# Hybrid encoder on one core: squares of the first norm on VectorE, two more banks for the third FFN tile, later constants, decays and masked scores on ScalarE

## The chip, the cores and the metric

One Trainium2 chip, one core. The metric is the device time of one execution in microseconds; three executions of the kernel before gave a median of 2577.45 us (2576.88 to 2578.72).

## What is computed

A two-layer encoder on 512 tokens of width 1024 in f32. Each layer is half an FFN, a mixer of three branches (SSD, S5, retention) with sigmoid gates, and half an FFN; every part starts with an RMS norm. From the reference, cut to what the change touches:

```
def rmsnorm(x, g):
    return x * lax.rsqrt(jnp.mean(x * x, axis=-1, keepdims=True) + EPS) * g
def swiglu(x, w_gate, w_up, w_down):
    return (jax.nn.silu(x @ w_gate) * (x @ w_up)) @ w_down
# per layer: x = x + 1/2 * swiglu(rmsnorm(x)); mixer; x = x + 1/2 * swiglu(rmsnorm(x))
# SSD, per chunk of 128 tokens and per head, each direction:
    scores = jnp.einsum('bclhn,bcshn->bhcls', cm, bm) * segsum_exp(da)
    y_diag = jnp.einsum('bhcls,bcshp->bclhp', scores, xd)
```

## The kernel before

x is kept transposed as eight tiles `x[k]` of 128 features by 512 tokens. Weights come in chunks: `wload` (L138 to L152) starts the DMA on SyncE into `wst`, ScalarE rounds it to fp32r (`whi`, L149), VectorE subtracts (`wlo`, L150); the pool has three buffers of each. `mm3` (L156 to L158) makes each product of three matmuls, high by high, high by low, low by high. The order in which each engine gets its instructions is set by the framework's scheduler from the program's text and its priorities; each engine runs its own list in order.

**The start.** `load_first` (L255) issues x and the first weights. `norm_k` (L164) scales x by the gain and splits it into `hh` (ScalarE, L170) and `hl` (VectorE, L171). `norm_sq` (L175) squares `x[k]`: k=0 on GpSimd (L180), the others on ScalarE into `sqk` (L183; tag `t_a`, three buffers), and GpSimd adds them to `sqsum` (L184). `norm_fin` (L186) splits the sum (L161, L162), sums over features by matmuls with ones (L194), takes the power on GpSimd (`rtd`, L199), scales the identity by it (`dg`, L202) and spreads it over the partitions by a matmul of ones by `dg` (L204), copied to `rbc` (L206). The `ffn` (L208) applies `rbc` only after a product: per tile m, gate and up product (24 matmuls each) go into two PSUM banks of tag "mm", which has four; then `gt` = gate product times `rbc` (L224, VectorE), Silu (L225, ScalarE), times `rbc` (L227, GpSimd), times the up product (L229, VectorE). So TensorE can do two tiles before `rbc` exists, and the third waits for a bank. `load_consts` (L124) loads `con` (identity, masks) and `tri`, casts two triangles of `tri` to fp32r (`ls_r` L131, `us_r` L133); `load_vecs2` (L277) loads small vectors and makes `hbg` (L281). The generator `side` (`s5_prep`, with the loads L712, L717, L866 on ScalarE's queue) is advanced by one step after each FFN tile, at a low priority.

**The SSD stage.** In `ssd` (L516), `stage_a(t)` makes the masked scores `gm` of a chunk t (L622, L626) and `stage_b(t)` (L640) does, per group g of four heads: `bm` = forward scores by step size (L644, GpSimd), plus the backward ones (four instructions, L647, VectorE); twice (forward, backward) `rb`, a triangle mask times the decay of each head, in a high part `dah` (L653, VectorE) and a low part `dal` (L653, GpSimd); four matmuls with `ls_r`, `us_r` (L657); Exp (`e`, L660, ScalarE); `e` by `bm` (L661, VectorE); four matmuls with `xs` (L664). There are eight such rounds a layer (four chunks, two groups). Between chunks `hook()` runs an S5 block (L997 to L1045: `za`, `zb`, scan and `h` on VectorE, `z`, `ia`, `ib` on GpSimd, products into `ps_pa`, `ps_pb`), and the gate projections (24 matmuls a tile, L1056, L1058) fill TensorE in between.

Of the kernel before, what the change touches and what calls it, by code (L numbers as in the profile page):

```python
# [101 lines left out]
class Core:  # L102
    def __init__(self, ctx, tc, consts):
# [17 lines left out]
        nc.vector.memset(self.nmh, -0.5)  # L121

    def load_consts(self):
        nc = self.nc  # L124
        nc.sync.dma_start(self.con, self.consts[:, :C_N])
        self.ones_r = self.c0.tile([P, 2], F32R, name="ones_r")
        nc.vector.tensor_copy(self.ones_r, self.ones[:, :2])
        tri = self.tp.tile([P, 2 * P], F32, tag="t_a", name="tri", bufs=3)
        nc.sync.dma_start(tri, self.consts[:, C_LS:C_LS + 2 * P])
        self.ls_r = self.c0.tile([P, P], F32R, name="ls_r")  # L130
        nc.vector.tensor_copy(self.ls_r, tri[:, :P])  # L131
        self.us_r = self.c0.tile([P, P], F32R, name="us_r")
        nc.vector.tensor_copy(self.us_r, tri[:, P:])  # L133
# [4 lines left out]
    def wload(self, src, nk, n, eng=None):  # L138
# [5 lines left out]
        for j, s_ in enumerate(srcs):  # L144
            (eng or nc.sync).dma_start(sv.rearrange("p (k n) -> p k n", k=nk)[:, :, j * wd:(j + 1) * wd],
                                       s_.rearrange("(k p) n -> p k n", p=P))
# [17 lines left out]
    def norm_k(self, k, gcol, sq=True):  # L164
# [5 lines left out]
        nc.scalar.activation(self.hh[k], x, AF.Copy, scale=g)  # L170
# [4 lines left out]
    def norm_sq(self, k):  # L175
        nc = self.nc
        x = self.x[k]
        if k == 0:
            self.sq = self.c1.tile([P, S], F32, tag="sqsum", name="sqsum")
            nc.gpsimd.tensor_tensor(self.sq, x, x, ALU.mult)  # L180
        else:
            t = self.tp.tile([P, S], F32, tag="t_a", name="sqk", bufs=3)
            nc.scalar.activation(t, x, AF.Square)  # L183
            nc.gpsimd.tensor_tensor(self.sq, self.sq, t, ALU.add)  # L184
# [23 lines left out]
    def ffn(self, ap, wg, wu, wd, after, side=iter(()), pre=None):  # L208
        nc = self.nc
        blocks = ((0, 10), (10, 22))  # L210
        for bi, (m0, m1) in enumerate(blocks):
            ah, al = [], []
            for m in range(m0, m1):
# [3 lines left out]
                pg = self.bank()  # L217
                for k in range(KD):
                    self.mm3(pg, gh[:, k], gl[:, k], self.hh[k], self.hl[k], k == 0, k == KD - 1)
                pu = self.bank()  # L220
# [33 lines left out]
    def load_first(self, i):  # L254
# [16 lines left out]
        nc.scalar.activation(warm, self.ones[:, :2], AF.Silu)  # L271
        for k in range(KD):
# [3 lines left out]
    def load_vecs2(self, i):  # L276
        nc = self.nc  # L277
        nc.sync.dma_start(self.vec2, i["vecs"][:, 108:])
        nc.sync.dma_start(self.s5d, i["s5ds"])
        self.hbg = self.c0.tile([P, 48], F32, name="hbg")  # L280
        nc.vector.tensor_scalar(self.hbg, self.vec[:, V_BG:V_BG + 48], 0.5, None, ALU.mult)  # L281
# [225 lines left out]
    def ssd(self, i, L, xs, hook=lambda: None):  # L507
# [4 lines left out]
        with self.tc.tile_pool(name="ssd", bufs=1) as sp:  # L512
# [126 lines left out]
            def stage_b(t, w_, gm):  # L639
                py = self.bank("sm")  # L640
                for g in range(2):
                    hs = slice(4 * g, 4 * g + 4)
                    bm = sp.tile([P, 4, P], F32, tag="bm", name="bm", bufs=2)
                    nc.gpsimd.tensor_tensor(bm, self.bc(gm[:, 0, g].unsqueeze(1), [P, 4, P]),  # L644
                                            self.bc(dt4[:, t, 0, hs].unsqueeze(2), [P, 4, P]), ALU.mult)
                    for h in range(4):
                        nc.vector.scalar_tensor_tensor(bm[:, h], gm[:, 1, g], dt4[:, t, 1, 4 * g + h:4 * g + h + 1],  # L647
                                                       bm[:, h], ALU.mult, ALU.add)
                    seg = self.bank("sm")
                    for d, m, lm in ((0, ui, self.ls_r), (1, li, self.us_r)):  # L650
                        rb = sp.tile([P, 2, 4, P], F32R, tag="rb", name="rb", bufs=2)
                        for j, s_ in enumerate((dah.bitcast(F32), dal)):
                            (nc.vector if j == 0 else nc.gpsimd).tensor_tensor(  # L653
                                rb[:, j], self.bc(m.unsqueeze(1), [P, 4, P]),
                                self.bc(s_[:, t, 8 * d + 4 * g:8 * d + 4 * g + 4].unsqueeze(2), [P, 4, P]), ALU.mult)
# [44 lines left out]
    def s5_params(self, i, L, keep, sp, sd):  # L700
# [9 lines left out]
        for nm in ("s5_lam_re", "s5_lam_im"):  # L710
            o = new(nm)
            nc.scalar.dma_start(o, i[nm][L])  # L712
# [3 lines left out]
        for d in range(2):  # L716
            nc.scalar.dma_start(ls[64 * d:64 * d + 64, :], i["s5_log_step"][L, d].partition_broadcast(64))  # L717
# [122 lines left out]
        with self.tc.tile_pool(name="s5c", bufs=1) as qp:  # L840
# [23 lines left out]
            for ri, nm in enumerate(("s5_c_re", "s5_c_im")):  # L864
                if ri == 0:
                    nc.scalar.dma_start(ct[:, 0], i[nm][L])  # L866
# [351 lines left out]
```

## Time and profile before

| | |
|---|---|
| median of 3 runs | 2577.45 us |
| the profiled execution | 2580.19 us (span 2578.4) |
| TensorE busy | 2538.3 us (98%) |
| VectorE / ScalarE / GpSimd busy | 59% / 34% / 25% |
| TensorE's granted clock, mean | 0.988 |

The busy share is a mean over the program: how an engine stands in a stretch is read from that stretch. TensorE's granted clock is given in parts of its full 2.4 GHz; at 0.50 it is the lower of its two levels, 1.2 GHz. A row in a timeline ends, in brackets, with the time its engine idled before it and what ended that.

### The profile page before, as it was taken

The page shows a single profiled execution, that of the slowest core. Times are in us where ns is not written, and L with a number is a line of the kernel's source. Part 1 is how long each engine was busy: PE and PEld are TensorE (multiplying, and loading weights), DVE is VectorE, ACT ScalarE, POOL GpSimd, SP SyncE. Part 2 cuts the span into 40 slices and gives each one's busy share as a digit, 9 for nine tenths or more (in the row PEclk, how much of TensorE's full clock was granted, in tenths as well). Part 3 has the DMA queues.
Part 4 walks back from the last instruction along what each step waited for, and adds up shares of the span by engine and source line. Part 5 has one row for each costly group of instructions (what it writes and reads, how often), then busy time and mean ns, then how long its engine had stood idle before and what let it go on. Part 6 is the DMA issues. An engine that isn't in the chain of part 4 may idle for free. (4 is left out here: it accounts for less than half of the span.)

```text
span 2578.4 us, 31738 instructions
## 1 busy us (share of the span) xinstructions
PE 2538.3 (98%) x12044; PEld 2104.0 (82%) x12044; DVE 1514.7 (59%) x2462; ACT 878.3 (34%) x1298; POOL 646.9 (25%) x636
## 2 busy tenths in 40 slices
PE   8999999999999999999999999999999999999998
PEld 6878887778888888888887888887878888888886
DVE  7746746897555644333486377478965556433433
ACT  4324433334333432222333243333343333322222
POOL 3203411462233221011112043105613323210110
PEclk9999999989999999999999999999899999999999
DMA  5434435342423433332334344454324234324322
GB/s 155 128 116 137 145 120 162 115 129 65 130 78 83 119 98 89 106 98 88 102 89 142 113 148 138 132 144 127 108 69 126 82 82 121 100 82 114 98 83 81
DMA packets 451832, 286.34 MB, mean 111 GB/s; under 512 B 29152, under 2 KB 435296, under 8 KB 451680
## 3 DMA queue, kind: packets, MB, share of 16 engines
q1 hardware_dynamic: 447456, 281.26, 36.7%
q10 hardware_dynamic: 4224, 3.06, 0.4%
q8 instruction: 95, 1.56, 0.2%
q14 instruction: 57, 0.47, 0.1%
HBM read 251.24 MB, written 29.88 MB: 109 GB/s over the span
## 5 line engine op out<-in xcount | busy, mean ns | idle before, releaser
L149 ACT ACTIVATE whi<-wst 128x1024 fp32r<-128x1024 f32 (+4 forms) x488 | 451.6, 927 | 1136.0 <-PE ps_mm L157 906.2
L156 PE MATMUL ps_mm<-hh,whi 128*128 128x512 f32 x1936 | 760.6, 393 | 6.4 <-ACT whi L149 3.7
L158 PE MATMUL ps_mm<-hh,wlo 128*128 128x512 f32 x1936 | 763.9, 395 | 2.6 <-DVE wlo L150 2.6
L157 PE MATMUL ps_mm<-hl,whi 128*128 128x512 f32 x1936 | 761.7, 394 | 0.0
L150 DVE TENSOR_TENSOR wlo<-wst,whi 128x1024 fp32r<-128x1024 f32 (+4 forms) x488 | 558.4, 1145 | 247.3 <-ACT whi L149 246.3
L156 PEld LDWEIGHTS ps_mm<-hh,whi 128*128 128x128 f32 x1936 | 366.2, 189 | 84.2 <-ACT whi L149 4.9
L158 PEld LDWEIGHTS ps_mm<-hh,wlo 128*128 128x128 f32 x1936 | 365.8, 189 | 79.4 <-DVE wlo L150 3.7
L157 PEld LDWEIGHTS ps_mm<-hl,whi 128*128 128x128 f32 x1936 | 365.9, 189 | 77.6 <-issue 1.7
L227 POOL TENSOR_TENSOR sr<-gt,rbc 128x512 f32<-128x512 f32 x88 | 149.1, 1696 | 817.9 <-ACT gt L225 817.9
L158 PE MATMUL ps_mm<-ah,wlo 128*128 128x512 f32 x704 | 275.6, 391 | 3.1 <-DVE wlo L150 3.1
L157 PE MATMUL ps_mm<-al,whi 128*128 128x512 f32 x704 | 274.6, 390 | 0.0
L156 PE MATMUL ps_mm<-ah,whi 128*128 128x512 f32 x704 | 274.1, 390 | 0.0
L229 DVE TENSOR_TENSOR a<-ps_mm,sr 128x512 f32<-128x512 f32 x88 | 60.4, 687 | 178.8 <-PE ps_mm L158 167.5
L158 PEld LDWEIGHTS ps_mm<-ah,wlo 128*128 128x128 f32 x704 | 132.4, 188 | 31.1 <-DVE wlo L150 3.9
L157 PEld LDWEIGHTS ps_mm<-al,whi 128*128 128x128 f32 x704 | 132.4, 188 | 28.2 <-DVE al L162 0.6
L156 PEld LDWEIGHTS ps_mm<-ah,whi 128*128 128x128 f32 x704 | 132.6, 188 | 27.9 <-ACT ah L161 0.7
L224 DVE TENSOR_TENSOR gt<-ps_mm,rbc 128x512 f32<-128x512 f32 x88 | 60.1, 686 | 139.7 <-PE ps_mm L158 139.6
L157 PE MATMUL ps_mm<-wlo,hh 128*128 128x512 f32 x320 | 126.3, 395 | 0.0
L156 PE MATMUL ps_mm<-whi,hh 128*128 128x512 f32 x320 | 125.9, 400 | 0.0
L158 PE MATMUL ps_mm<-whi,hl 128*128 128x512 f32 x320 | 125.5, 392 | 0.0
L245 DVE SCALAR_TENSOR_TENSOR x<-ps_mm,x 128x512 f32<-128x512 f32 x64 | 44.3, 692 | 133.7 <-PE ps_mm L158 133.4
L184 POOL TENSOR_TENSOR sqsum<-sqsum,sqk 128x512 f32<-128x512 f32 x42 | 67.4, 1606 | 191.0 <-ACT sqk L183 190.7
(395 smaller groups left out, 3257.2 us busy)
## 6 DMA issues: line engine op xcount, KB each, us to landing
wst<-in_ffn_w_gate SPq DMA_DIRECT2D x87, 512.0 KB, 3.7
wst<-in_ffn_w_up SPq DMA_DIRECT2D x87, 512.0 KB, 3.7
wst<-in_w_in SPq DMA_DIRECT2D x74, 512.0 KB, 3.7
wst<-in_ffn_w_down SPq DMA_DIRECT2D x64, 384.0 KB, 3.1
wst<-in_ffn_w_down SPq DMA_DIRECT2D x64, 320.0 KB, 3.1
wst<-in_w_in SPq DMA_DIRECT2D x64, 256.0 KB, 3.0
mat<-sd SPq DMA_DIRECT2D x12, 896.0 KB, 5.1
sd<-mat SPq DMA_DIRECT2D x12, 768.0 KB, 5.0
```

The costliest lines, as they stand in the source:

```text
L149: nc.scalar.activation(hi[:, :nk * n], sv, AF.Copy)
L150: nc.vector.tensor_tensor(lo[:, :nk * n], sv, hi[:, :nk * n].bitcast(F32), ALU.subtract)
L156: mm(out, lh, rh, start=first, stop=False)
L157: mm(out, lh, rl, start=False, stop=False)
L158: mm(out, ll, rh, start=False, stop=last)
L184: nc.gpsimd.tensor_tensor(self.sq, self.sq, t, ALU.add)
L224: nc.vector.tensor_tensor(gt, pg, self.rbc, ALU.mult)
L227: nc.gpsimd.tensor_tensor(sr, gt, self.rbc, ALU.mult)
L229: nc.vector.tensor_tensor(a, pu, sr, ALU.mult)
L245: nc.vector.scalar_tensor_tensor(self.x[d], pd, 0.5, self.x[d], ALU.mult, ALU.add)
```

## The change

1. The seven additions of the first norm's squares go from GpSimd to VectorE. The square of k=0 stays on GpSimd.
2. In the first FFN, the third tile's two products go to the banks "pa" and "pb" (one each, otherwise used by the S5 blocks) rather than "mm".
3. Only the identity (128 columns of `con`) is loaded at the start, after x. The rest of `con`, `tri`, `vec2`, `s5d` are loaded from the second step of `side`; the casts `ls_r`, `us_r` and `hbg` come after `rbc`. The loads of `side` on ScalarE's queue wait for the last `hh`.
4. In `stage_b`, the forward `bm` is made by four activations of 128x128 (Copy with a scale) in place of one GpSimd instruction, `dah`'s part of `rb` by four activations in place of one VectorE instruction, and `dal`'s part by VectorE in place of GpSimd. Per layer: 32 + 64 more activations, 16 + 8 fewer GpSimd instructions, as many VectorE ones as before (16).

```diff
@@ class Core
+        self.ls_r = self.c0.tile([P, P], F32R, name="ls_r")
+        self.us_r = self.c0.tile([P, P], F32R, name="us_r")
+    def load_consts(self):
+        nc = self.nc
+        with self.tc.issue_after(self.last_w.ins):
+            nc.sync.dma_start(self.con[:, P:], self.consts[:, P:C_N])
+            tri = self.tp.tile([P, 2 * P], F32, tag="t_a", name="tri", bufs=3)
+            nc.sync.dma_start(tri, self.consts[:, C_LS:C_LS + 2 * P])
+        with self.tc.issue_after(self.after_norm.ins):
+            nc.vector.tensor_copy(self.ls_r, tri[:, :P])
+            nc.vector.tensor_copy(self.us_r, tri[:, P:])
@@ norm_sq
-            nc.gpsimd.tensor_tensor(self.sq, self.sq, t, ALU.add)
+            (eng or nc.gpsimd).tensor_tensor(self.sq, self.sq, t, ALU.add)
@@ ffn
-                pg = self.bank()
+                wide = pre and m == 2
+                pg = self.bank("pa" if wide else "mm")
-                pu = self.bank()
+                pu = self.bank("pb" if wide else "mm")
@@ load_first
+        nc.sync.dma_start(self.con[:, :P], self.consts[:, :P])
         for k in range(KD):
             self.norm_k(k, V_N1, False)
@@ stage_b
-                    nc.gpsimd.tensor_tensor(bm, self.bc(gm[:, 0, g].unsqueeze(1), [P, 4, P]),
-                                            self.bc(dt4[:, t, 0, hs].unsqueeze(2), [P, 4, P]), ALU.mult)
                     for h in range(4):
+                        nc.scalar.activation(bm[:, h], gm[:, 0, g], AF.Copy, scale=dt4[:, t, 0, 4 * g + h:4 * g + h + 1])
@@ stage_b, for each direction d
-                        for j, s_ in enumerate((dah.bitcast(F32), dal)):
-                            (nc.vector if j == 0 else nc.gpsimd).tensor_tensor(
-                                rb[:, j], self.bc(m.unsqueeze(1), [P, 4, P]),
-                                self.bc(s_[:, t, 8 * d + 4 * g:8 * d + 4 * g + 4].unsqueeze(2), [P, 4, P]), ALU.mult)
+                        c0 = 8 * d + 4 * g
+                        for h in range(4):
+                            nc.scalar.activation(rb[:, 0, h], m, AF.Copy, scale=dah[:, t, c0 + h:c0 + h + 1].bitcast(F32))
+                        nc.vector.tensor_tensor(rb[:, 1], self.bc(m.unsqueeze(1), [P, 4, P]),
+                                                self.bc(dal[:, t, c0:c0 + 4].unsqueeze(2), [P, 4, P]), ALU.mult)
@@ s5_prep: s5_lam_re, s5_lam_im; also s5_log_step and s5_c_re
+            with self.tc.issue_after(self.last_hh.ins):
+                nc.scalar.dma_start(o, i[nm][L])
@@ hybrid_encoder_kernel
-    c.load_consts()
-    c.load_vecs2(i)
     for k in range(KD):
-        c.norm_sq(k)
+        c.norm_sq(k, tc.nc.vector)
     c.norm_fin()
+    def first_side(sd):
+        yield
+        c.load_consts()
+        c.load_vecs2(i)
+        yield
+        yield from c.s5_prep(i, 0, sd)
```

How the lists of instructions move is shown at three places. The first is ScalarE's list in the first microseconds (`hh` and `sqk` as above, `x_75` is x[0], `x_76` x[1] and so on). Before:

```order
L149 ACTIVATE whi<-wst 128x512
L170 ACTIVATE hh_136<-x_76,vec 128x512
L717 DMA ls<-in_s_log_step 64x24
L170 ACTIVATE hh_140<-x_77,vec 128x512
L717 DMA ls<-in_s_log_step 64x24
L149 ACTIVATE whi<-wst 128x512
L866 DMA ct<-in_s_c_re 128x384
L170 ACTIVATE hh_144<-x_78,vec 128x512
L170 ACTIVATE hh_148<-x_79,vec 128x512
L149 ACTIVATE whi<-wst 128x512
L170 ACTIVATE hh_152<-x_80,vec 128x512
L183 ACTIVATE sqk<-x_76 128x512
```

After (the changed kernel's L152, L173 and L186 are L149, L170 and L183 of before):

```order
L173 ACTIVATE hh_138<-x_75,vec 128x512
L173 ACTIVATE hh_142<-x_76,vec 128x512
L186 ACTIVATE sqk<-x_76 128x512
L152 ACTIVATE whi<-wst 128x512
L173 ACTIVATE hh_146<-x_77,vec 128x512
L186 ACTIVATE sqk<-x_77 128x512
L152 ACTIVATE whi<-wst 128x512
L173 ACTIVATE hh_150<-x_78,vec 128x512
L186 ACTIVATE sqk<-x_78 128x512
L173 ACTIVATE hh_154<-x_79,vec 128x512
L186 ACTIVATE sqk<-x_79 128x512
L152 ACTIVATE whi<-wst 128x512
```

The squares now alternate with the splits and stand ahead of the first rounding of a weight, and the small loads are gone from between them.

The second is VectorE's list from the copy to `rbc` (L206, now L209) to the first `gt` (L224, now L228); `s_lam_re`, `pe`, `hp` and `t` are small tiles of `s5_prep`. Before:

```order
L206 COPY rbc<-ps_sm 128x512
L719 TENSOR_SCALAR s_lam_re<-s_lam_re 128x24
L477 TENSOR_SCALAR pe_306<-ls 128x24
L753 MEMSET hp 128x1
L772 TENSOR_TENSOR t_459<-s_lam_im 128x24
L224 TENSOR_TENSOR gt<-ps_mm,rbc 128x512 x2
```

After:

```order
L209 COPY rbc<-ps_sm 128x512
L135 CAST ls_r<-tri 128x128
L136 CAST us_r<-tri 128x128
L287 TENSOR_SCALAR hbg<-vec 128x48
L727 TENSOR_SCALAR s_lam_re<-s_lam_re 128x24
L483 TENSOR_SCALAR pe_453<-ls 128x24
L761 MEMSET hp 128x1
L780 TENSOR_TENSOR t_606<-s_lam_im 128x24
L228 TENSOR_TENSOR gt<-ps_mm,rbc 128x512 x2
```

The two casts and `hbg` stand between `rbc` and `gt`. The load of `tri` stands on SyncE behind the gate and up weights of the fourth tile and takes a `t_a` buffer that the product of ones by `dg` (now L207) reads; on TensorE that product stands two matmuls into the third tile, before it stood ahead of the third tile.

The third is ScalarE's list in one chunk's two rounds of `stage_b` (L1045/L1054 is the S5 block's Gelu, `gate` a gate tile's Tanh). Before:

```order
L660 ACT_TABLE_LOAD
L660 ACTIVATE e<-ps_sm 128x512
L1045 ACT_TABLE_LOAD
L1045 ACTIVATE yg<-ps_pb 128x256
L660 ACT_TABLE_LOAD
L660 ACTIVATE e<-ps_sm 128x512
L149 ACTIVATE whi<-wst 128x1024
L1058 ACTIVATE gate<-gate,hbg 128x512
L149 ACTIVATE whi<-wst 128x1024
```

After:

```order
L659 ACTIVATE rb<-con,dah 128x128 x4
L666 ACT_TABLE_LOAD
L666 ACTIVATE e<-ps_sm 128x512
L659 ACTIVATE rb<-con,dah 128x128 x4
L651 ACTIVATE bm<-gm,dt 128x128 x2
L1054 ACT_TABLE_LOAD
L1054 ACTIVATE yg<-ps_pb 128x256
L651 ACTIVATE bm<-gm,dt 128x128 x2
L659 ACTIVATE rb<-con,dah 128x128 x4
L666 ACT_TABLE_LOAD
L666 ACTIVATE e<-ps_sm 128x512
```

Four activations for a part of `rb` stand directly ahead of each Exp, with four for the other direction and four for the next `bm` between two of them; the number of table loads is the same.

## Rows read from the trace of the kernel before

**Rows 1.** The page's busy time by engine: us (share of span) xinstructions.

```profile
PE 2538.3 (98%) x12044; PEld 2104.0 (82%) x12044; DVE 1514.7 (59%) x2462; ACT 878.3 (34%) x1298; POOL 646.9 (25%) x636
```

**Rows 2.** Busy time by stretch: start:end us; per engine busy (xinstructions); PEclk; DMA share; GB/s.

```profile
0.00:50.00 50.00, 41.76 (x158) 32.77 (x159) 33.54 (x64) 22.45 (x33) 18.07 (x17) 0.93 0.55 168
476.00:600.00 124.00, 117.31 (x604) 98.05 (x602) 113.07 (x178) 43.37 (x53) 78.43 (x81) 0.92 0.39 120
```

**Rows 3.** Timeline, TensorE, 0-45 us: start, duration, what; [idle before <-releaser].

```profile
12.32 0.50 PE L156 MATMUL ps_mm<-hh,whi 128*128 128x512 f32 x1 [1.45 <-ACT whi L149]
...
21.92 0.50 PE L156 MATMUL ps_mm<-hh,whi 128*128 128x512 f32 x1 [1.37 <-ACT whi L149]
...
23.47 0.80 PE L158 MATMUL ps_mm<-hh,wlo 128*128 128x512 f32 x1 [0.82 <-DVE wlo L150]
...
36.57 1.12 PE L204 MATMUL ps_sm<-dg,ones 128*128 128x512 f32 x2
40.33 0.64 PE L156 MATMUL ps_mm<-hh,whi 128*128 128x512 f32 x1 [2.64 <-DVE gt L224]
```

**Rows 4.** Timeline, ScalarE, 0-45 us.

```profile
11.64 0.63 ACT L149 ACTIVATE whi<-wst 128x512 fp32r<-128x512 f32 x1 [2.89 <-DMA wst<-in_ffn_w_up]
...
20.29 0.63 ACT L183 ACTIVATE sqk<-x 128x512 f32<-128x512 f32 x1 [3.05 <-DVE us_r L133]
...
26.81 0.63 ACT L161 ACTIVATE sqh<-sqsum 128x512 fp32r<-128x512 f32 x1 [2.01 <-POOL sqsum L184]
```

**Rows 5.** Timeline, GpSimd, 0-45 us.

```profile
13.58 6.59 POOL L184 TENSOR_TENSOR sqsum<-sqsum,sqk 128x512 f32<-128x512 f32 x4 [8.96 <-ACT sqk L183]
```

**Rows 6.** Timeline, VectorE, 0-45 us.

```profile
17.05 1.31 DVE L131 CAST ls_r<-tri 128x128 fp32r<-128x128 f32 x1
...
38.73 0.68 DVE L206 COPY rbc<-ps_sm 128x512 f32<-128x512 f32 x1
```

**Rows 7.** DMA issues, 0-40 us: out<-in queue xcount, KB each, median us to landing.

```profile
tri<-in_consts SPq DMA_DIRECT2D x1, 128.0 KB, 4.9
```

**Rows 8.** Stretches at half clock, columns as in rows 2.

```profile
23.47:26.88 3.41, 3.41 (x8) 2.76 (x9) 3.00 (x2) 1.40 (x3) 3.23 (x2) 0.50 0.53 156
40.54:43.95 3.41, 3.41 (x9) 2.64 (x9) 3.38 (x10) 1.00 (x2) 2.54 (x2) 0.50 0.43 129
528.64:535.47 6.83, 6.39 (x23) 5.52 (x23) 5.63 (x15) 2.63 (x4) 3.65 (x5) 0.50 0.58 204
573.01:586.66 13.65, 12.68 (x46) 11.48 (x47) 12.29 (x22) 5.71 (x9) 6.29 (x6) 0.50 0.37 106
1805.23:1812.06 6.83, 6.60 (x20) 5.54 (x21) 5.63 (x15) 1.09 (x2) 4.63 (x5) 0.50 0.32 126
1846.19:1856.43 10.24, 9.23 (x33) 8.18 (x34) 9.09 (x18) 5.38 (x9) 3.61 (x4) 0.50 0.36 90
```

**Rows 9.** TensorE's waits, 520-600 us: line <- waited for: us total, times, longest.

```profile
PE ps_pb L1043 <- DVE h L1037: 1.7, 2, 1.3
PE ps_sm L664 <- DVE e L661: 1.5, 2, 1.0
PE ps_sm L631 <- DVE gm L626: 1.3, 1, 1.3
```

**Rows 10.** TensorE's waits, 1800-1885 us.

```profile
PE ps_pb L1043 <- DVE h L1037: 2.0, 2, 1.3
PE ps_sm L664 <- DVE e L661: 1.5, 4, 0.7
```

**Rows 11.** Tile rb, whole span: count, ns min/median/max, first and last start.

```profile
L653 POOL TENSOR_TENSOR rb<-con,dal x32: 1041/1483/2031, 478.1 to 1875.3; 128x512 fp32r<-128x512 f32 x32
L653 DVE TENSOR_TENSOR rb<-con,dah x32: 677/1220/1783, 479.6 to 1879.9; 128x512 fp32r<-128x512 f32 x32
```

**Rows 12.** Tile e, 500-610 us, columns as in rows 11.

```profile
L661 DVE TENSOR_TENSOR e<-e,bm x7: 678/679/1524, 529.7 to 606.4; 128x512 f32<-128x512 f32 x7
```

**Rows 13.** Timeline, ScalarE, at 628 us.

```profile
628.27 0.61 ACT L469 ACTIVATE bh<-ps_sm,vec 128x128 fp32r<-128x128 f32 x2
```

More of the change, by code (lines that the diff above doesn't have):

```diff
@@ L121, in __init__ @@
         nc.vector.memset(self.nmh, -0.5)
+        self.ones_r = self.c0.tile([P, 2], F32R, name="ones_r")
+        nc.vector.tensor_copy(self.ones_r, self.ones[:, :2])
+        self.ls_r = self.c0.tile([P, P], F32R, name="ls_r")
+        self.us_r = self.c0.tile([P, P], F32R, name="us_r")
+        self.hbg = self.c0.tile([P, 48], F32, name="hbg")
     def load_consts(self):
         nc = self.nc
[L125 to L133, printed above, removed]
+        with self.tc.issue_after(self.last_w.ins):
[5 more added lines that the diff above has]
+            nc.vector.tensor_copy(self.us_r, tri[:, P:])
     def bank(self, tag="mm"):
@@ L144, in wload @@
         for j, s_ in enumerate(srcs):
-            (eng or nc.sync).dma_start(sv.rearrange("p (k n) -> p k n", k=nk)[:, :, j * wd:(j + 1) * wd],
+            self.last_w = (eng or nc.sync).dma_start(sv.rearrange("p (k n) -> p k n", k=nk)[:, :, j * wd:(j + 1) * wd],
                                        s_.rearrange("(k p) n -> p k n", p=P))
@@ L169, in norm_k @@
         g = self.vec[:, gcol + k:gcol + k + 1]
-        nc.scalar.activation(self.hh[k], x, AF.Copy, scale=g)
+        self.last_hh = nc.scalar.activation(self.hh[k], x, AF.Copy, scale=g)
         nc.vector.scalar_tensor_tensor(self.hl[k], x, g, self.hh[k].bitcast(F32), ALU.mult, ALU.subtract)
@@ L173, in norm_k, with norm_sq @@
             self.norm_sq(k)
-    def norm_sq(self, k):
+    def norm_sq(self, k, eng=None):
         nc = self.nc
@@ L277, in load_vecs2 @@
         nc = self.nc
[L278 to L281, printed above, removed]
+        with self.tc.issue_after(self.last_w.ins):
+            nc.sync.dma_start(self.vec2, i["vecs"][:, 108:])
+            nc.sync.dma_start(self.s5d, i["s5ds"])
+        with self.tc.issue_after(self.after_norm.ins):
+            nc.vector.tensor_scalar(self.hbg, self.vec[:, V_BG:V_BG + 48], 0.5, None, ALU.mult)
     def final_k(self, d, ap, g, out):
@@ L711, in s5_params @@
             o = new(nm)
-            nc.scalar.dma_start(o, i[nm][L])
+            with self.tc.issue_after(self.last_hh.ins):
+                nc.scalar.dma_start(o, i[nm][L])
             lam.append(o)
@@ L716, in s5_params @@
         for d in range(2):
-            nc.scalar.dma_start(ls[64 * d:64 * d + 64, :], i["s5_log_step"][L, d].partition_broadcast(64))
+            with self.tc.issue_after(self.last_hh.ins):
+                nc.scalar.dma_start(ls[64 * d:64 * d + 64, :], i["s5_log_step"][L, d].partition_broadcast(64))
         with self.tc.issue_after(self.after_norm.ins):
@@ L865, in s5_params @@
                 if ri == 0:
-                    nc.scalar.dma_start(ct[:, 0], i[nm][L])
+                    with self.tc.issue_after(self.last_hh.ins):
+                        nc.scalar.dma_start(ct[:, 0], i[nm][L])
                     continue
@@ L1155, in hybrid_encoder_kernel @@
         with tc.tile_pool(name="ffa", bufs=1) as ap:
-            side = c.s5_prep(i, L, sd)
+            side = c.s5_prep(i, L, sd) if L else first_side(sd)
             c.xd = c.dr.tile([KD, P, S], F32, tag="xd", name="xd")
```

## The prediction

> **What bounds the kernel now.** I read the page's busy times first: TensorE is busy for 2538.3 of 2578.4 us [rows 1], so most of the time is matmuls that the change leaves alone, and what it can win is TensorE's idle time and the time at its lower clock. The windows say where to look [rows 2]: in the first 50 us TensorE works 41.8 us at a mean granted clock of 0.93, and in the 124 us around the SSD stage of layer 1 it works 117.3 us at 0.92, while VectorE is busy for 113.1 and GpSimd for 78.4. The rest of the program has few such places.
>
> At the start, TensorE's timeline shows five gaps after its first product [rows 3]: 1.45, 1.37 and 0.82 us for weights not yet rounded or subtracted, and 2.64 us before the third tile, for a bank that `gt` frees once `rbc` is there; the norm's own matmul at 36.57 closes the second tile. Behind them: ScalarE's rounding at 11.64 waited for a DMA; a square at 20.29 waited 3.05 us for a buffer that VectorE's cast of `tri` held, and the next rounding stood behind it; the split of the sum at 26.81 waited for GpSimd [rows 4], whose four additions in a row took 6.59 us, 1.65 each [rows 5]. `rbc` is copied at 38.73 [rows 6]. After two of the gaps the clock is at 0.50 for 3.41 us [rows 8]: 8 wide matmuls in that time, 0.43 each, so 0.21 each at the full clock, and a tile of 48 lasts between 10 and 11 us.
>
> In the SSD stage TensorE waits for VectorE: for `h`, `e` and `gm`, 4.5 us in layer 1 [rows 9] and at least 3.5 in layer 2 [rows 10]. Four stretches at half clock go with it, 6.83, 13.65, 6.83 and 10.24 us, 37.55 in all [rows 8]; at the full clock half of it, 18.8 us, would be saved. Why VectorE is late is in the tiles' rows: the `dah` part of `rb` takes from 0.68 to 1.78 us for the same work, at the median 1.22, while GpSimd works at the `dal` part for 1.48 [rows 11], and the product `e` takes 0.68 at the median and 1.52 at worst [rows 12]. VectorE and GpSimd stretch each other here.
>
> **The change part by part.** All sums are against the profiled execution, 2580.2 us (span 2578.4 and 1.8 around it), which is 2.7 above the median; a saving is taken as the same for both.
>
> *The start.* Seven additions leave GpSimd, at 1.65 us, for VectorE. An instruction of that size with both inputs in SBUF takes VectorE 0.68 us [rows 12], so 4.8 us are added to an engine busy for 33.5 of 50 [rows 2], spread between roundings, and the sum is done when the last square is, about 20 us rather than 26.8. `tri` no longer holds a buffer, so the 3.05 us wait goes and with it the gap of 1.37. The 0.82 behind it (VectorE late with a subtraction after the casts and the wait) goes too. Of the 1.45 us, which a DMA ended, I take half, since `con`, `tri` and the small loads no longer share the queues with the first weights, 0.75; bounds 0 and 1.45. The 2.64 us go, because the third tile has banks of its own. The two stretches at half clock stood directly behind gaps that go; their cost is half of 2 x 3.41, so 3.4. Against that, the first rounding now stands behind two `hh` and a square rather than one `hh`: two activations of about 0.6 more, less what the weight's DMA covers, 0.55. Sum: 0.75 + 1.37 + 0.82 + 2.64 + 3.4 - 0.55 = 8.4 us saved. Bounds: 6 with no share of the DMA's gap and one stretch half left, 10 with all.
>
> A new wait lies there: the casts of `tri` now stand on VectorE ahead of `gt`. `tri` is loaded into a buffer that the product of ones by `dg` must have read, two matmuls into the third tile. The second tile ends at 36.57 less 0.75 + 1.37 + 0.82 + 1.7, plus 0.55, about 32.5; that product is at 33; `tri` lands 4.9 us after its issue [rows 7], at 38; two casts at up to 1.31 each [rows 6], and `gt` starts at 40.5 or a little later. The fourth tile needs its bank when the third ends, 10 to 11 us after 32.5, at 43. So the wait is covered by some 2 us, and if SyncE issues `tri` later than that, because it waits behind the fourth tile's weights, the cover is gone: each us more is a gap, and a stretch at half clock (1.7 us) comes with it. The other loads that move land long before their use.
>
> *The SSD stage.* GpSimd loses 16 `rb` parts a layer, 1.48 us each, so 24 us, and eight `bm` products more; VectorE keeps 16 `rb` instructions, of the same shape. If they run at their undisturbed 0.68 in place of 1.22, VectorE gains 16 x 0.54 = 8.6 us a layer, and its other instructions (`e`, the roundings, `h`) gain as their partners go. That leaves it at about 100 of 124 or below. ScalarE gets 96 activations a layer. Two such of 128x128 with a scale from SBUF took 0.61 us together, about 0.37 for one and 0.25 more for the next [rows 13]; 96 x 0.26 = 25 us, on 43.4 of 124 [rows 2]. It stands at 55% then, and would be full at 0.84 us each (80.6 / 96). The Trainium skill, "ScalarE: Activation LUTs", section "What ACT_TABLE_LOAD costs", gives an activation 186 ns and 93 more for each pointer operand, plus 0.833 ns a column, less an overlap of 93: estimated from it, 0.39 for one and 0.29 for the next, so 28 us a layer in place of 25, and the row agrees.
>
> How much of TensorE's 8.0 us of waits and 18.8 us of slow clock that returns isn't in any row. The bounds are 0, if the waits merely change their name, and 26.8. I take 7 of the 8.0 us of waits, because `h` and `e` are late behind instructions that were stretched, and keep one wait for `e` a layer, since four activations (1.1 us) stand ahead of Exp. Of the slow clock I take half, 9.4: the four stretches stand among the waits of rows 9 and 10, and I keep those that stand at the waits that stay. Together 16.4.
>
> *Elsewhere* the lists hardly move: 0, with 4 us either way for gaps shifting.
>
> Sum: 8.4 + 16.4 = 24.8 us saved: 2555.4 against the profiled 2580.2, and on the median 2577.45 - 24.8 = 2552.7, so **2553 us**.
>
> **The rivals.** *Only the start wins.* GpSimd keeps `ia`, `ib`, `xw`, `z` and more, some 78.4 - 24 - 9 = 45 of 124 us, and the instructions of VectorE with two inputs in SBUF, the `dal` part among them, go on meeting them; then the waits for `h` and `e` stay and the slow clock with them. For it: `h` reads `ia` and `ib`, which stay on GpSimd. Against: half of what stretched VectorE at `e` and `h` was `rb` itself. Time: 2577.4 - 8.4 = 2569. The Trainium skill, "SBUF — State Buffer", section "Who interferes with whom", says that such an instruction contends with a GpSimd instruction reading SBUF, by an exclusive lock with the loser blocked; the 0.68 against 1.78 us agrees with it, and by that rule what stays on GpSimd goes on doing harm.
>
> *All of the slow clock goes.* If VectorE is early by some us a round, the gaps vanish together: 8.4 + 26.8 + 4 elsewhere, 2538 us.
>
> *Slower: ScalarE becomes the engine waited for.* Exp stands behind four activations, 1.1 us, where before `rb` was made on two engines at once. If TensorE's filling work is used up at that point in each of the 16 rounds, that is 17.6 us of waits, and four further stretches of 3.41 at half clock, 6.8: 24.4 lost, 8.4 won at the start, so 2577.4 + 16 = 2593. It decides when the chain of masks to Exp is longer than the gate products between, or when an activation takes 0.84 us and ScalarE is full. Against it: a round lasts 12.8 us (seven `e` from 529.7 to 606.4 [rows 12]), and ScalarE would need 4.5 + 3.1 of it. The Trainium skill, "ScalarE: Activation LUTs", section "Rules for kernel authors", says to multiply on VectorE rather than ScalarE; by it, this half of the change goes the wrong way.
>
> *The start wins nothing.* `tri` comes late, 2 to 4 us of gap with a stretch of 1.7, and the SSD stage stays: 2572 to 2575, close to no change.
>
> **How the numbers follow.** Chances: the forecast 0.60, only the start 0.21, all of the slow clock 0.10, slower 0.05, nothing at the start 0.04. The range runs from 2541, near the case in which all goes, to 2570, which holds the case of the start alone; it leaves out half of the best case, the last two and some of the start's own spread. The forecast's own range is 2545 to 2561. A change within 0.2% (5 us, what a measurement of this kernel can tell from nothing) is 2572.3 to 2582.6: the last case and the edge of the second, 0.06. Faster 0.89, slower 0.05.
>
> **What would show it.** Right: no gap of TensorE above 1 us between 10 and 50 us, the third tile's end near 43 to 44 us (before, it began at 40.33 and had some 12 us to go), `gt` before 43; the `rb` part on VectorE at about 0.7 us; 128x128 activations at 0.25 to 0.3 start to start; fewer and shorter stretches at 0.50 around 573, 1805 and 1846. Wrong: `rb` at 1.2 us still, TensorE waiting for `h` as before; ScalarE named as the releaser of TensorE's waits in the SSD stage; a wait of VectorE for `tri`, with TensorE waiting for `gt` at the fourth tile.

## The result, and the profile after

The changed kernel took 2562.35 us at the median of four executions (2552.71 to 2565.37), against 2578.09 for the kernel before: a ratio of 0.9932 (0.9904 to 0.9960), 15.7 us less. The forecast was 24.8 us less, 2553, with a range from 2541 to 2570. Five further executions of the changed kernel gave 2562.05 (2559.44 to 2562.60), a ratio of 0.9933 (0.9921 to 0.9944).

The execution that was profiled first took 2552.71 us, the forecast to within 0.3, but it is the fastest of nine; the others lie between 2559 and 2566. It had a mean granted clock of 0.994, the other eight 0.990 to 0.993 (before, 0.986 to 0.991 over all its executions). So its profile is read here beside that of a second execution, 2562.05 us, called *again* below. What the lower clock costs in all can be estimated as one minus the mean clock, times the span: before 0.012 x 2578 = 31 us, the first profile 0.006 x 2551 = 15, *again* 0.008 x 2560 = 20 (rounded clocks, so to 1 or 2 us).

The page's busy times and the two stretches of [rows 1, 2], first profile:

```profile
PE 2517.2 (99%) x12044; PEld 2088.5 (82%) x12044; DVE 1486.5 (58%) x2469; ACT 934.2 (37%) x1490; POOL 571.6 (22%) x581
```

```profile
0.00:50.00 50.00, 46.42 (x200) 38.12 (x201) 36.12 (x95) 24.73 (x38) 7.07 (x10) 0.97 0.63 188
476.00:600.00 124.00, 117.47 (x638) 97.31 (x638) 104.67 (x185) 73.92 (x151) 49.06 (x59) 0.99 0.38 116
```

GpSimd went from 78.4 to 49.1 us around the SSD stage, VectorE from 113.1 to 104.7, ScalarE from 43.4 to 73.9.

**The start.** TensorE's timeline now has two gaps at the very start and none from 8 to 123 us; these rows answer to [rows 3]:

```profile
6.77 0.50 PE L159 MATMUL ps_mm<-hh,whi 128*128 128x512 f32 x1 [2.25 <-ACT whi L152]
...
7.77 0.79 PE L161 MATMUL ps_mm<-hh,wlo 128*128 128x512 f32 x1 [0.27 <-DVE wlo L153]
```

VectorE's timeline after, to be read beside [rows 6], with the last of the seven additions, the casts of `tri`, and `gt` of the first two tiles and of the fourth:

```profile
16.43 0.68 DVE L187 TENSOR_TENSOR sqsum<-sqsum,sqk 128x512 f32<-128x512 f32 x1
...
33.84 0.68 DVE L209 COPY rbc<-ps_sm 128x512 f32<-128x512 f32 x1
34.44 0.22 DVE L135 CAST ls_r<-tri 128x128 fp32r<-128x128 f32 x1
...
35.07 1.28 DVE L228 TENSOR_TENSOR gt<-ps_mm,rbc 128x512 f32<-128x512 f32 x2
...
50.03 0.68 DVE L228 TENSOR_TENSOR gt<-ps_mm,rbc 128x512 f32<-128x512 f32 x1
```

The fourth tile's `gt` in the kernel before:

```profile
58.85 0.68 DVE L224 TENSOR_TENSOR gt<-ps_mm,rbc 128x512 f32<-128x512 f32 x1
```

Between these two rows lie 8.8 us. The casts stand directly behind `rbc` and took 0.22 us, not 1.31; VectorE did not wait for `tri`.

**Part of it is given back.** TensorE's waits from 118 to 140 us, before and after, and the stretch at half clock there after the change (before it was 3.41 us, with TensorE busy throughout):

```profile
PE ps_mm L158 <- DVE wlo L150: 2.2, 1, 2.2
```

```profile
PE ps_mm L159 <- ACT ah L164: 2.4, 1, 2.4
PE ps_mm L161 <- DVE wlo L153: 1.9, 1, 1.9
```

```profile
126.92:137.16 10.24, 7.83 (x19) 5.65 (x18) 7.85 (x10) 1.99 (x3) 4.13 (x4) 0.50 0.30 89
```

Here the first down-projection begins and needs VectorE, which is at the S5 preparation. There are 2.1 us more of waits, and TensorE works for 7.83 us at the low clock where it was 3.41, of which half, 2.2 us, is lost: 4.3 us in this execution. In *again* it was 3.0 us of waits and as much time at half clock as before.

**The SSD stage.** The tile `rb` over the whole span, as in [rows 11], and TensorE's waits in the first stage, as in [rows 9], first profile:

```profile
L659 ACT ACTIVATE rb<-con,dah x128: 384/388/406, 473.5 to 1852.1; 128x128 fp32r<-128x128 f32 x128
L660 DVE TENSOR_TENSOR rb<-con,dal x32: 677/684/1244, 474.0 to 1851.7; 128x512 fp32r<-128x512 f32 x32
```

```profile
PE ps_pb L1052 <- DVE h L1046: 4.7, 2, 2.8
PE ps_sm L637 <- DVE gm L632: 0.5, 1, 0.5
PE ps_pa L1018 <- DMA mat<-sd: 0.4, 1, 0.4
PE ps_sm L670 <- DVE e L667: 0.3, 1, 0.3
```

VectorE's `rb` runs at its undisturbed 0.68 us, and the waits for `e` and `gm` are nearly gone. But the wait for `h` has grown from 1.7 to 4.7 us, so that the three sum to 5.5 us in this stage where [rows 9] have 4.5. In both stages together they were 8.8 us before ([rows 9, 10] and 0.8 for `gm`), 8.7 in the first profile and 10.4 in *again*: next to none of the waiting came back. The longest wait, 2.80 us, in the timeline of the first profile (GpSimd, VectorE, TensorE, one after the other):

```profile
581.21 1.70 POOL L1039 TENSOR_TENSOR ia<-it,mat 128x256 f32<-128x256 f32 x1
582.88 0.77 POOL L1040 TENSOR_TENSOR ib<-it,mat 128x256 f32<-128x256 f32 x1
```

```profile
580.64 1.69 DVE L153 TENSOR_TENSOR wlo<-wst,whi 128x1024 fp32r<-128x1024 f32 x1
582.25 2.06 DVE L652 SCALAR_TENSOR_TENSOR bm<-gm,dt,bm 128x128 f32<-128x128 f32 x4
584.24 0.41 DVE L1045 TENSOR_TENSOR h<-ia,ib 64x252 f32<-64x252 f32 x1
584.66 0.42 DVE L1046 TENSOR_TENSOR h<-ia,ib 64x252 f32<-64x252 f32 x1
```

```profile
585.23 0.41 PE L1052 MATMUL ps_pb<-h,mat 128*128 128x64 f32 x2 [2.80 <-DVE h L1046]
```

`ia` took 1.70 us beside two VectorE instructions with both inputs in SBUF; the same product takes 0.73 at best. `ib` was done at 583.65, `h` began at 584.24, behind VectorE's four `bm` instructions. But this is not why the wait grew: in the same S5 block of the kernel before, where TensorE did not wait, the second `ia` was stretched as much:

```profile
591.76 1.72 POOL L1030 TENSOR_TENSOR ia<-it,mat 128x256 f32<-128x256 f32 x1
```

What differs stands further back on the chain to `h`, where VectorE begins the block's `za` from TensorE's first products (`ps_pa`). TensorE's last of these and VectorE's first `za` after the change, then the first `za` before it:

```profile
569.23 0.33 PE L1018 MATMUL ps_pa<-uc,mat 128*128 128x64 f32 x2
574.27 0.41 DVE L1028 TENSOR_TENSOR za<-ps_pa,mat 64x256 f32<-64x256 f32 x1
```

```profile
584.49 0.42 DVE L1019 TENSOR_TENSOR za<-ps_pa,mat 64x256 f32<-64x256 f32 x1 [0.24 <-PE ps_pa L1009]
```

Before, VectorE stood waiting for the products and began at once. Now it is busy with other instructions of its list and begins 4.7 us after them (with part 4 alone too, not with the start alone), and `h` is ready 15.5 us after them in place of 13.1. The list of TensorE also has less to do in between: 61 matmuls in place of 64 in this block. At the stage's other wait for `h`, 1.9 us, `h` is even ready earlier, 14.5 us after the block's first products where it was 16.1 without a wait; but 62 matmuls stand between where 75 stood. In both blocks a part of them ran at half clock before ([rows 8]), which gave `h` time.

**The same wait, two clocks.** The stretch from this wait on in the first profile, then the one behind the same wait (2.75 us, it ends at 583.30) in *again*, and the one there in the second stage:

```profile
582.42:592.66 10.24, 7.44 (x49) 6.73 (x49) 10.15 (x21) 6.85 (x21) 1.22 (x2) 1.00 0.18 52
```

```profile
584.98:595.22 10.24, 10.24 (x38) 9.08 (x38) 6.94 (x13) 7.18 (x18) 0.00 (x0) 0.50 0.09 26
1847.91:1861.56 13.65, 13.29 (x46) 11.86 (x47) 8.99 (x17) 7.09 (x18) 0.00 (x0) 0.50 0.07 20
```

In *again* the two SSD stages hold 3.41 + 10.24 + 3.41 + 13.65 = 30.7 us at half clock, before it was 37.55 [rows 8]; in the first profile it was 3.41 + 6.83 = 10.2. Half of the difference is 10.2 us. The spans of the two executions differ by 9.4 us; smaller differences, in the waits for `h` of the second stage (2.8 and 4.7 us) and at the first down-projection, go both ways.

### The profile page after: what moved, and what is told of

Same layout as the page of the kernel before. It is cut to its first block, busy times and chain, and to the rows that moved or that the text cites. A ratio compares the mean times of both kernels' runs of the same rounds, so it can differ in the third digit from the quotient of the medians.

```text
span 2550.9 us, 31890 instructions
## 1 busy us (share of the span) xinstructions
PE 2517.2 (99%) x12044; PEld 2088.5 (82%) x12044; DVE 1486.5 (58%) x2469; ACT 934.2 (37%) x1490; POOL 571.6 (22%) x581
## 4 chain that ended last, share of the span: by engine, by line
PE 84%; DVE 9%; issue 2%; POOL 2%; DMA 1%; ACT 1%; SPq 1%; ACTq 0%; DVEq 0%; POOLq 0%
PE ps_mm L161 25%; PE ps_mm L159 25%; PE ps_mm L160 25%; DVE wlo L153 2%; PE ps_sm L427 1%; DVE bm L652 1%; PE ps_pa L435 1%; PE ps_sm L392 1%; POOL ia L1039 1%; PE ps_pa L434 1%; DMA sd<-mat 0%; DVE za L1028 0%; DVE zb L1029 0%; PE ps_sm L965 0%; PE ps_pa L1018 0%
## 5 line engine op out<-in xcount | busy, mean ns | idle before, releaser
L152 ACT ACTIVATE whi<-wst 128x1024 fp32r<-128x1024 f32 (+4 forms) x488 | 451.5, 927 | 1099.1 <-PE ps_mm L160 877.2
L161 PE MATMUL ps_mm<-hh,wlo 128*128 128x512 f32 x1920 | 753.7, 393 | 1.1 <-DVE wlo L153 1.1
L159 PE MATMUL ps_mm<-hh,whi 128*128 128x512 f32 x1920 | 751.6, 392 | 2.2 <-ACT whi L152 2.2
L160 PE MATMUL ps_mm<-hl,whi 128*128 128x512 f32 x1920 | 753.1, 392 | 0.0
L228 DVE TENSOR_TENSOR gt<-ps_mm,rbc 128x512 f32<-128x512 f32 x87 | 59.4, 687 | 138.5 <-PE ps_mm L161 138.5
L187 POOL TENSOR_TENSOR sqsum<-sqsum,sqk 128x512 f32<-128x512 f32 x35 | 55.7, 1591 | 180.7 <-ACT sqk L186 180.7
```

Source lines behind the costliest of these rows:

```text
L152: nc.scalar.activation(hi[:, :nk * n], sv, AF.Copy)
L159: mm(out, lh, rh, start=first, stop=False)
L160: mm(out, lh, rl, start=False, stop=False)
L161: mm(out, ll, rh, start=False, stop=last)
L187: (eng or nc.gpsimd).tensor_tensor(self.sq, self.sq, t, ALU.add)
L228: nc.vector.tensor_tensor(gt, pg, self.rbc, ALU.mult)
```

## The experiments

Times on different chips are compared by their ratio to the kernel before on the same chip.

**The changed kernel once more** (no edit).

> The changed kernel itself, unaltered, for more executions of it. Theory A (both halves save, and single executions lose some us to stretches at half clock that come and go): its times again lie over 10 us apart, between about 2552 and 2566, and time and mean granted clock move together, 0.001 of clock for 2.5 us. Theory B (the first profiled execution was a stray one): all executions lie within 3 us of 2563.

2562.05 us, ratio 0.9933 (0.9921 to 0.9944), all within 3.2 us. Theory B was nearer: the first profiled execution was a stray one, and most of what it has ahead is clock, as shown above.

**The start alone** (parts 1 to 3; `stage_b` as before):

```diff
-                        nc.scalar.activation(bm[:, h], gm[:, 0, g], AF.Copy, scale=dt4[:, t, 0, 4 * g + h:4 * g + h + 1])
+                    nc.gpsimd.tensor_tensor(bm, self.bc(gm[:, 0, g].unsqueeze(1), [P, 4, P]),
+                                            self.bc(dt4[:, t, 0, hs].unsqueeze(2), [P, 4, P]), ALU.mult)
...
-                            nc.scalar.activation(rb[:, 0, h], m, AF.Copy, scale=dah[:, t, c0 + h:c0 + h + 1].bitcast(F32))
-                        nc.vector.tensor_tensor(rb[:, 1], self.bc(m.unsqueeze(1), [P, 4, P]),
+                            (nc.vector if j == 0 else nc.gpsimd).tensor_tensor(
```

> Parts 1 to 3 of the change with stage_b as before it. Theory A (the start gives 8 to 9 us): about 2569, with the SSD stretches at half clock as before. Theory B (the start's gain is lost again at the first down-projection): 2574 to 2578. Theory C (all of the measured 15.7 us comes from the start): about 2562.

2570.80 us, ratio 0.9973 (0.9962 to 0.9984): 7 to 8 us, between theories A and B. At the fourth tile's `gt` (49.54 us) the kernel is 9.3 us ahead, and the SSD stages have their time at half clock as before (20.48 and 17.07 us, and 10.24 ahead of the second).

**Part 4 alone**, on the kernel before (the last edit the other way round):

```diff
-                            (nc.vector if j == 0 else nc.gpsimd).tensor_tensor(
+                            nc.scalar.activation(rb[:, 0, h], m, AF.Copy, scale=dah[:, t, c0 + h:c0 + h + 1].bitcast(F32))
+                        nc.vector.tensor_tensor(rb[:, 1], self.bc(m.unsqueeze(1), [P, 4, P]),
...
```

> Part 4 alone, on the kernel before. Theory A (part 4 gives 12 to 18 us): 2560 to 2566, rb on VectorE at 0.7 us and less than 8 us at half clock in the two SSD stages. Theory B (the forecast's first rival, only the start wins): 2576 to 2579, waits for h and e as before. Theory C (ScalarE late): above 2580.

2568.72 us, ratio 0.9957 (0.9943 to 0.9972): 10 to 11 us, less than theory A, and clearly not B or C. Its executions lie 12 us apart (2561.60 to 2573.48). The profiled one, 2570.63 us, has none of theory A's small rest of slow clock: 20.48 us at half clock in each stage, and the wait of 2.8 us for `h` in both. Start and part 4 add up: 8.0 + 10.1 = 18.1, together 16.8 on that chip.

**The low part of `rb` back on GpSimd:**

```diff
-                        nc.vector.tensor_tensor(rb[:, 1], self.bc(m.unsqueeze(1), [P, 4, P]),
+                        nc.gpsimd.tensor_tensor(rb[:, 1], self.bc(m.unsqueeze(1), [P, 4, P]),
```

> The changed kernel with the dal part of rb back on GpSimd (16 instructions a layer), the rest as changed. Theory A (what stretches VectorE is GpSimd's work beside its two-input instructions): GpSimd's rb takes 1.0 to 1.5 us again, the e products and the roundings on VectorE are longer, and about a third to a half of part 4's gain is lost: 2566 to 2570. Theory B (VectorE only had too many instructions): VectorE has 16 fewer a layer, and the time is that of the changed kernel or below, 2555 to 2562.

2559.10 us, ratio 0.9923 (0.9910 to 0.9936); theory B. Moving this product to VectorE brought nothing by itself, or cost 3 us; the intervals overlap. GpSimd's part took 1.05 us at the median in place of 1.48, now that VectorE no longer makes its half at the same time.

**The S5 preparation two steps earlier:**

```diff
     def first_side(sd):
-        yield
         c.load_consts()
         c.load_vecs2(i)
-        yield
         yield from c.s5_prep(i, 0, sd)
```

> The changed kernel without the two empty steps ahead of the S5 preparation: its steps run two FFN tiles earlier, as in the kernel before, and the constants with the first of them. In the changed kernel TensorE waits at 123.6 us (1.9 us, a weight's low part) and at 128.8 (2.4, the split of a), where before there was one wait of 2.2. Theory A (the preparation's VectorE work, two tiles later than before, now meets the start of the first down-projection): one of the two waits goes with the half-clock stretch behind it, 3 to 5 us less than the changed kernel, about 2558. Theory B (TensorE comes there 9 us earlier and simply finds VectorE not done): the waits stay within 1 us in sum, 2560 to 2564, or more if the large constants delay the second tile's weights.

2561.72 us, ratio 0.9938 (0.9923 to 0.9954); theory B. The waits at the first down-projection were 2.1 and 3.2 us. In VectorE's list this work did not move up to there, whatever the step's number; so the edit tested little of theory A.

**The S5 blocks' `ib` on VectorE:**

```diff
-            gp.tensor_tensor(zb[:, ri], it[:, ri], rt[:, 1], ALU.mult)
+            v.tensor_tensor(zb[:, ri], it[:, ri], rt[:, 1], ALU.mult)
```

> The changed kernel with the S5 blocks' ib products (two of 128x256 a block) on VectorE in place of GpSimd. In the changed kernel TensorE still waits for h, 1.9 and 2.8 us in each SSD stage. Theory A (ia and ib in a row on GpSimd, stretched by VectorE, set the end of h): the longest wait for h falls below 1.5 us, and with it the half-clock stretch behind; 3 to 8 us less than the changed kernel, 2554 to 2559. Theory B (h waits in VectorE's list behind the bm instructions): the waits for h stay at 2 to 3 us or grow, and the time is 2561 or more.

2550.36 us (2548.26 to 2551.35), ratio 0.9890 (0.9877 to 0.9902): theory A, and more than it said: some 11 us below the changed kernel, and below its best execution. TensorE's waits in the first stage (512 to 592 us), and the stretch of [rows 2], of this kernel and then of *again*:

```profile
PE ps_sm L670 <- DVE e L667: 1.9, 3, 0.7
PE ps_pb L1052 <- DVE h L1046: 1.8, 2, 1.3
PE ps_sm L637 <- DVE gm L632: 0.9, 2, 0.5
```

```profile
476.00:600.00 124.00, 119.22 (x649) 98.60 (x649) 105.86 (x195) 74.64 (x152) 40.50 (x49) 1.00 0.37 116
```

```profile
476.00:600.00 124.00, 117.79 (x607) 97.56 (x606) 103.21 (x182) 72.36 (x149) 49.03 (x59) 0.94 0.37 114
```

The waits sum to 4.6 us where *again* has 5.6, so little of the 11 us is waiting. It is the clock: 1.00 in this stretch, where *again* has 0.94, and no stretch at half clock in the rounds of either SSD stage (3.41 us at 613.75 come behind the first); the mean clock is 0.997, by the estimate above 8 us lost in place of 20. The wait of 2.8 us is gone, but not by a shorter chain alone: in that block `za` begins 3.0 us after the first products in place of 4.7, `h` is ready after 14.9 us in place of 15.5, and TensorE's list has 72 matmuls in between in place of 61.

**`ib` on VectorE and nothing else**, on the kernel before (the same edit):

> The kernel before with nothing changed but the S5 blocks' ib products on VectorE. Theory A (the wait for h behind GpSimd's ia and ib is what costs, with or without part 4): 2564 to 2570, the longest wait for h below 1.2 us. Theory B (part 4 has to make room on VectorE first, which is busy for 113 of 124 us there): 2576 to 2582, waits for e and gm grow.

2568.75 us, ratio 0.9969 (0.9958 to 0.9981). The time is theory A's, the waits are theory B's; from 512 to 610 us:

```profile
PE ps_sm L664 <- DVE e L661: 4.3, 3, 2.1
PE ps_sm L631 <- DVE gm L626: 1.1, 1, 1.1
```

No wait for `h` is left there, but VectorE, busy for 115.5 of the 124 us from 476 on, is late with `e`. In the changed kernel the same edit is worth about as much or more.

**Both, `ib` on VectorE and the low part on GpSimd** (the two edits):

> The changed kernel with ib on VectorE and the dal part of rb back on GpSimd, both of which were the same or better alone. Theory A (VectorE is what must be relieved, whatever it reads): VectorE gets some 8 us back a stage, no wait above 1 us, 2547 to 2550. Theory B (GpSimd beside VectorE's two-input instructions stretches both): e and h are late again, 2552 to 2558.

2554.27 us, ratio 0.9906 (0.9891 to 0.9921): theory B, not better than `ib` alone. The longest wait for `h` was 1.8 us, and 6.83 us at half clock came back in each stage. With `ib` gone from GpSimd, the move of the low part to VectorE seems to pay, some 4 us; the intervals just overlap.

**The forward `bm` back on GpSimd:**

```diff
-                        nc.scalar.activation(bm[:, h], gm[:, 0, g], AF.Copy, scale=dt4[:, t, 0, 4 * g + h:4 * g + h + 1])
+                    nc.gpsimd.tensor_tensor(bm, self.bc(gm[:, 0, g].unsqueeze(1), [P, 4, P]),
+                                            self.bc(dt4[:, t, 0, hs].unsqueeze(2), [P, 4, P]), ALU.mult)
```

> The changed kernel with the forward bm product back on GpSimd (8 instructions a layer in place of 32 activations); rb stays on ScalarE and VectorE. Theory A (GpSimd's S5 products ia and ib set the end of the long waits for h, so work put back on GpSimd lengthens them): waits for h of 2.5 us or more, 3 to 6 us more than the changed kernel, 2565 to 2568. Theory B (rb is what mattered in part 4, bm is neutral): within 3 us of 2562. Theory C (the bm activations made VectorE's bm instructions run ahead of h, which is what h waits for): waits for h below 1.5 us, 2552 to 2558.

2563.01 us against 2574.95 for the kernel before on that chip: ratio 0.9966 (0.9952 to 0.9979), some 8 us above the changed kernel. It is slower, as theory A said, but not by its mechanism: TensorE's waits became shorter, and yet the clock fell. With more work on GpSimd and `ia` still stretched to 1.72 us, the wait of 2.8 us for `h` is gone: VectorE begins that block's `za` 0.3 us after the first products, and `h` is ready after 11.8 us. Its waits from 512 to 592 us, then the 3.41 us ahead of a stretch at half clock and that stretch:

```profile
PE ps_pa L1019 <- DMA mat<-sd: 1.3, 1, 1.3
PE ps_pb L1053 <- DVE h L1047: 1.0, 1, 1.0
```

```profile
559.28:562.69 3.41, 2.22 (x11) 1.31 (x9) 3.27 (x6) 0.92 (x1) 0.45 (x1) 1.00 1.05 274
562.69:572.93 10.24, 10.24 (x40) 9.59 (x41) 7.16 (x16) 4.28 (x9) 3.30 (x4) 0.50 0.58 186
```

In the kernel with `ib` on VectorE a like stretch, after which the clock stayed at 1.00:

```profile
533.20:536.60 3.40, 2.05 (x10) 1.45 (x9) 3.34 (x10) 1.43 (x2) 0.55 (x1) 1.00 0.38 103
```

TensorE was idle for as long in the second, and did no more. So the length of a wait, or the idle time in these 3.4 us, doesn't tell whether the clock falls.

**The additions back on GpSimd:**

```diff
-        c.norm_sq(k, tc.nc.vector)
+        c.norm_sq(k)
```

> The changed kernel with the seven additions of the first norm back on GpSimd; the constants stay late and the third tile keeps its own banks. Theory A (the additions' place decides when rbc is there, but the third tile no longer waits for it): rbc is 5 to 8 us later than in the changed kernel (33.8), and TensorE waits for gt at the fourth tile, up to 3 us. Theory B (the two banks alone bring the start's gain): rbc later, no wait of TensorE above 1 us before 50 us, the same time as the changed kernel within 2 us.

2564.39 us, ratio 0.9943 (0.9930 to 0.9956); neither theory. `rbc` came at 38.06, 4.2 us later, and TensorE did not wait for `gt` at all. It waited for `hl`, which VectorE makes beside GpSimd's additions, in 1.26 us at the median in place of 0.74; its waits from 0 to 60 us:

```profile
PE ps_mm L160 <- DVE hl L174: 2.2, 2, 1.5
PE ps_mm L159 <- ACT whi L152: 1.6, 1, 1.6
...
PE ps_mm L161 <- DVE wlo L153: 0.8, 1, 0.8
```

So with the banks there, what the additions' move brings is not the earlier `rbc` but a VectorE that GpSimd does not disturb; in the total 2 to 3 us, within the interval.

**The third tile in the usual banks:**

```diff
-                wide = pre and m == 2
+                wide = False
```

> The changed kernel with the third tile in the usual four banks. Theory A (the banks are worth the 2.6 us wait and its half-clock stretch): TensorE waits 2 to 4 us for gt at the third tile, 3 to 5 us more than the changed kernel. Theory B (with the additions on VectorE rbc is early enough): no such wait, the same time within 2 us.

2564.15 us, ratio 0.9944 (0.9929 to 0.9959). Theory A at the spot: TensorE waits for `gt` at the third tile, with 3.41 us at half clock behind it; from 0 to 60 us:

```profile
PE ps_mm L159 <- DVE gt L228: 3.2, 1, 3.2
PE ps_mm L159 <- ACT whi L152: 1.7, 1, 1.7
...
```

But the waits at the first down-projection shrink to 1.2 and 1.0 us, with no stretch at half clock, and in the total the banks are worth some 3 us, not clear of the interval. TensorE arrives there later.

**ScalarE's new work twice:**

```diff
                         nc.scalar.activation(bm[:, h], gm[:, 0, g], AF.Copy, scale=dt4[:, t, 0, 4 * g + h:4 * g + h + 1])
+                        nc.scalar.activation(bm[:, h], gm[:, 0, g], AF.Copy, scale=dt4[:, t, 0, 4 * g + h:4 * g + h + 1])
...
                             nc.scalar.activation(rb[:, 0, h], m, AF.Copy, scale=dah[:, t, c0 + h:c0 + h + 1].bitcast(F32))
+                            nc.scalar.activation(rb[:, 0, h], m, AF.Copy, scale=dah[:, t, c0 + h:c0 + h + 1].bitcast(F32))
```

> The changed kernel with each of the 96 activations of part 4 done twice a layer, so that ScalarE has some 27 us more in each SSD stage (about 100 of 124). The forecast's slower rival (ScalarE becomes the engine waited for once it is nearly full, or because four activations stand ahead of Exp): waits for e of 1 to 2 us in most of 16 rounds, 2575 to 2600. The other theory (the gate products cover it): ScalarE's load shows in no wait above 1 us, and the time is within 4 us of the changed kernel's 2562.

2567.74 us, ratio 0.9958 (0.9945 to 0.9972), 6 us above the changed kernel and between the two theories. With ScalarE busy for 96.7 of 124 us, the waits for `e` in a stage are 1.9 us in two, none in most rounds. The new wait stands behind the last round of each stage, where the first split of the part that follows (`bl`, VectorE) is late. ScalarE is not full at that point (in the first stage it idles for 3.8, 1.3 and 1.6 us in the 10 us before), so how its doubled work leads to this wait is not shown; TensorE's waits from 1870 to 1890 us:

```profile
PE ps_sm L471 <- DVE bl L476: 5.6, 1, 5.6
PE ps_mm L159 <- issue: 1.3, 1, 1.3
PE ps_sm L471 <- DVE xs L673: 0.8, 1, 0.8
```

## Why the prediction was right or wrong

The direction and the range held; the centre was 9 us too low at the median. The first profiled execution met it by luck, as its clock shows.

*The start, 8.4 us.* Right in size and in its reasons: 8.8 us at the fourth tile. The prediction speaks of five gaps and lists four; its sum uses the four. Within it, the whole of the DMA's 1.45 us went (I had taken half), the first product came 1.0 us later rather than 0.55 (6.77 against 5.76), and 3.41 us at half clock are new near 8 us, though not in every kernel with this start. The hazard of `tri` did not arise: it was there by 34.44 (forecast 38), and without GpSimd beside it a cast took 0.22 us. What I left out is the place where the gain is spent again: with TensorE 9 us earlier at the first down-projection, 3 to 4.3 us go there. The run with the start alone still ended 7 to 8 us ahead. Its profile wins 3.5 us back between 1250 and 1640 us, where the kernel before waits 2.7 us for a weight's low part and 1.4 for `kt` (a small tile of the S5 preparation) and this one 0.6 in all; why these waits go is open.

*The SSD stage, 16.4 us.* Measured, 10 to 11 alone. The durations were right: `rb` at 0.68 us, GpSimd at 49 us (forecast 45), VectorE at 104.7 (about 100). ScalarE's activations stand 0.29 us apart within a group of four (1.27 us for four, 0.39 for one), where I took 0.26 from [rows 13]; the 0.29 worked out from the Trainium skill ("ScalarE: Activation LUTs", section "What ACT_TABLE_LOAD costs") was nearer (for the two of [rows 13] its figures give 0.68 us, and the row has 0.61, so the two agree less well than I said). The step that failed is "I take 7 of the 8.0 us of waits, because `h` and `e` are late behind instructions that were stretched". It held for `e`, whose waits fell from 3.0 to 0.3 us over both stages. But those for `h` grew from 3.7 to 7.5 us, in *again* to 9.3, and nothing of the 7 came back. `h` does read `ia` and `ib`, which stayed on GpSimd and are stretched by VectorE in turn, as the first rival had said; but `ia` was stretched to 1.72 us before as well, and the version with `bm` on GpSimd has it so without the wait. What the rows show instead is VectorE's `za` 4.7 us late in the block of the longest wait, and fewer matmuls between a block's first products and `h` in TensorE's list. The forecast had no term for TensorE's list in the stage, nor for a TensorE that reaches `h` sooner at the full clock. The rule of the Trainium skill cited with that rival ("SBUF — State Buffer", section "Who interferes with whom") fits the 1.70 us of `ia` against 0.73.

*Half of the slow clock, 9.4 us.* In the four stretches I had counted it was too much for the usual execution: *again* has 30.7 us at half clock in the two stages, a gain of 3.4 us; the first profile gains 13.7 there. Another part of the gain lies where I had counted nothing: 10.24 us at half clock from 1774.51 on, ahead of the second stage's rounds, behind waits of 0.5 us for `h` and 0.6 for a state. The run with the start alone still has them (10.24 us at 1765 us); with part 4 alone, and in both profiles of the changed kernel, this wait for `h` and the stretch are gone, 5 us. So in *again* the SSD stages gain 8.5 us by the clock, near the 9.4 but by another sum, and nothing by the waits.

*Rivals.* "Only the start wins" is refuted as a whole by the run of part 4 alone; it was right that the waits for `h` stay, though not, by the rows above, for its reason. "All of the slow clock goes" needed one more edit: with `ib` on VectorE it went in both stages, at 2550. "Slower" would need more ScalarE than there is: even the doubled work cost 6 us, and at another place than Exp. "The start wins nothing" did not happen.

*What stays open.* Each edit also changes the lists that the scheduler makes, for every engine, and no run holds the lists fixed; so how much of a difference between two versions is an engine's load and how much is another order is not shown, for `ib` on VectorE above all. Nor is why the clock falls at one wait and not at another. Executions of one kernel differ in it by up to 10 us, and the version with `bm` on GpSimd has less waiting and more time at half clock. That a run of short products (64 columns) beside the waits has a part in it would fit some of the stretches; no run tested it.

## What to carry to other kernels

A wait bears the name of the last tile on a chain, and its cause can lie further back: here `h` was named, its stretched inputs `ia` and `ib` looked like the reason, and a comparison with the kernel before showed them as long as ever and `za`, four steps earlier, late. Compare the chain before and after, and the two lists, before putting a wait down to an engine. One more product moved (here two instructions a block) was then worth as much as the whole part, nearly all of it through the clock. A gain early in the program arrives at the next fixed obstacle earlier; follow the lead in the trace from place to place before adding it up. And before believing one profile, run the kernel several times: its best execution met the forecast, its median did not.

## What the runs showed of the hardware

One kernel's first four executions lay 12.7 us apart (2552.71 to 2565.37), at mean granted clocks from 0.994 to 0.990. The same wait of 2.8 us at the same place of the program was followed once by the full clock and once by 10.24 us at half clock. A cast of 128x128 took 1.31 us beside GpSimd's additions and 0.22 without them.
